# Causal mask of a tile's scores: from a matmul into their bank to VectorE's maximum

## The chip, the core and the metric

One core of a Trainium2 chip runs one layer of a hybrid decoder. The core has five engines, each with its own queue in program order: TensorE (PE; its weight loads are listed as PEld), VectorE (DVE), ScalarE (ACT), GpSimd (POOL) and SyncE (SP, which here issues DMAs alone). TensorE writes only to the eight banks of PSUM (128 partitions by 512 floats each); the others read them out. The metric is device time in microseconds, lower is better.

## What is computed

The layer takes 512 tokens of width 1024. Its first half projects them and runs two groups of heads side by side: a gated recurrence (HGRN2) and a sparse attention (NSA) with a compressed, a selected and a window branch. With 512 tokens both the selected and the window branch come out as plain causal attention, with different keys and values:

```python
m = kpos <= tc[None, None, :, None, None]
sc = jnp.where(m[:, :, None], sc, NEG)
p = jax.nn.softmax(...)
return jnp.einsum('bgrqnl,bgqnld->bgrqd', p.astype(vg.dtype), vg)
```

```python
mw = (kpos <= qpos) & (qpos - kpos < WIN) & (kpos >= 0)
pw = jax.nn.softmax(jnp.where(mw, sw, NEG), axis=-1)
```

There are 8 query heads of 64, in 2 groups with a key head each. The second half of the layer is a gated MLP of width 2816 with a short convolution.

## The kernel before

Tokens are cut into four tiles of 128, i = 0 to 3. Tile i attends to the tiles 0 to i, so a row of its scores has W = (i + 1) * 128 columns. Attention (L1060 and on) is a generator over units. For tiles 0 and 1 a unit is one head with both branches, 2W columns in one bank; for tiles 2 and 3 (the third and fourth) it is one head and one branch, `bs` of length 1, W = 384 or 512 columns. That makes 16 units in each tile of 2 and 3. In between stand a few units of the compressed branch (`h is None`).

Step s of the generator does, in this order: `scores` of unit s; a yield; `flip` of unit s - 4 (LAG = 4); `expo` of unit s; `weigh` of unit s - 1; a yield; and every fourth step `values` of four units.

- `scores` (L969 to L983): two matmuls of float32r inputs, L977 and L978, put the row's scores into a bank S (the keys are kept as a high and a low part). A third, L979, adds the causal mask for the last 128 columns: its weights are an identity, its moving operand `causb`, both bf16, 0 or -1e30 in each element. VectorE's reduction (L981) finds the row's maximum mx, negated.
- `expo` (L985 to L999): ScalarE takes the exponent of S + mx out of the bank, into a tile pt in SBUF, and sums the row (L998).
- `weigh`: at the second of two heads VectorE turns the sums into weights (L1012, L1013) and the rows of both heads are scaled: by VectorE for one branch (L1020), by ScalarE for the other (L1018).
- `flip` (L1029): TensorE transposes pt, 128 columns at a time, into a bank F; ScalarE copies it out to pT (L1036).
- `values` (L1057): products with the values, into a bank oT. `cmp_values` is its counterpart (L1042) in the compressed branch.

`emit` interleaves the generators by hand-set weights. Beside attention run, at 190 to 290 us: projections (`proj_T`, three matmuls a piece through `mm3`, L137 to L139, into a bank pT, with weights that ScalarE and VectorE split into a high part whi, L133, and a low part wlo, L134); the recurrence in levels (`hg_levels`: lev, hgA, hgQ, hgK, hgtot, hgE, L1100 to L1164); and the modulation rows (L1268 to L1287). The order of each engine's queue is the order in which Python emits, so a yield decides what stands beside what.

Banks come from one pool of eight (`PS`); a tile is handed to a later one when its last reader in program order is known. Tiles of more than 256 floats such as pt come from a pool of eight buffers (`TMP`), shared with hgE, hvT and others.

`causb` is made by GpSimd at L1386, ahead of the projections of the keys; GpSimd then computes the roots of the norms (L360).

Of the kernel before, what the change touches and what calls it, by code (L numbers as in the profile page):

```python
# [11 lines left out]
BF16 = mybir.dt.bfloat16  # L12
I32 = mybir.dt.int32
U8 = mybir.dt.uint8
AF = mybir.ActivationFunctionType
ALU = mybir.AluOpType
# [3 lines left out]
P = 128  # L20
# [41 lines left out]
C_CAUS = C_CMASK + NT * 32  # L62
# [30 lines left out]
def hybrid_layer_kernel(ctx: ExitStack, tc: tile.TileContext, d: dict, out: bass.AP, dbg=None):  # L93
    nc = tc.nc
    ve, sc, gp, pe, sp = nc.vector, nc.scalar, nc.gpsimd, nc.tensor, nc.sync

    cst = ctx.enter_context(tc.tile_pool(name="cst", bufs=1))
# [10 lines left out]
    def nm(s):  # L108
        uid[0] += 1
        return f"{s}_{uid[0]}"  # L110
# [4 lines left out]
    def PS(s="ps"):  # L115
        return psum.tile([P, 512], F32, tag="b", name=nm(s))

    def TMP(shape, dt=F32, tag="tmp"):
        n = 1
        for a in shape[1:]:  # L120
            n *= a
        if n > 256:
            return tp.tile(shape, dt, tag="t2", name=nm(tag), bufs=8)
        return tp.tile(shape, dt, tag="t1", name=nm(tag), bufs=4)

    def SM(shape, tag, dt=F32):
        return sm.tile(shape, dt, tag=tag, name=nm(tag))
# [8 lines left out]
    def mm3(o, ah, al, bh, bl, start, stop):  # L136
        pe.matmul(o, ah, bh, start=start, stop=False, skip_group_check=True)  # L137
        pe.matmul(o, ah, bl, start=False, stop=False, skip_group_check=True)  # L138
        pe.matmul(o, al, bh, start=False, stop=stop, skip_group_check=True)  # L139
# [116 lines left out]
    def next_parts(more=True, g=False):  # L256
        if not ahead:
            piece(g)
        w = ahead.pop(0)
        if more:  # L260
            piece()
        return w
# [4 lines left out]
    cb = cst.tile([P, C_COLS], F32, name="cb")  # L267
# [334 lines left out]
    for k in range(KT):  # L602
        h = hT[k]
        n = k + 1
# [28 lines left out]
        for i in range(NT if k else 0):  # L633
            sl = slice(i * P, (i + 1) * P)
# [5 lines left out]
        for j in range(2):  # L640
            sl = slice(j * P, (j + 1) * P)
# [67 lines left out]
    def prep(steps):  # L709

        for step in steps:
            for f, u in [(w[0], w[1:]) for w in step.split()]:
                if f == "s":
                    units[u] = squares(makers[u[0]](int(u[1])))
                elif f == "r":
                    root(units[u])
                elif f == "n":
                    norm(units[u])
                elif f == "f":
                    units[u][0][4](units[u])  # L720
                else:
                    units[u][0][5](units.pop(u))
            yield
# [24 lines left out]
    QS = []  # L748
# [22 lines left out]
    KK = {}  # L771
# [3 lines left out]
    def proj_kv():  # L775
        kva.extend(PS("kva") for _ in range(NT))
        for a in range(0, KT, 2):
            hi, lo = next_parts()
            for b in range(2):
                k = a + b  # L780
                for i in range(NT):
                    sl = slice(i * P, (i + 1) * P)
                    mm3(kva[i], hT[k][:, 0, sl], hT[k][:, 1, sl], hi[:, b], lo[:, b], k == 0, k == KT - 1)
                    if i % 2:
                        yield
# [159 lines left out]
    def cmp_scores(i):  # L945
        ps = PS("S")
        for h in range(8):
            g = h // 4
            pe.matmul(ps[:, h * 64:h * 64 + 64], QS[i][:, h], KC[:, g], start=True, stop=True)
        pv = ps.rearrange("p (h e n) -> p h e n", h=8, e=2)  # L950
        s3 = TMP([P, 8, 32], tag="sc3")
        ve.tensor_tensor(s3, pv[:, :, 0],
                         cb[:, C_CMASK + 32 * i:C_CMASK + 32 * i + 32].unsqueeze(1)
                         .to_broadcast([P, 8, 32]), ALU.add)
        ve.tensor_tensor(s3, pv[:, :, 1], s3, ALU.add)
        mx = SM([P, 8], "cmx")
        ve.tensor_reduce(mx, s3, AX.X, ALU.max)
        ve.tensor_tensor(s3, s3, mx.unsqueeze(2).to_broadcast([P, 8, 32]), ALU.subtract)
        return s3
# [9 lines left out]
    def scores(u):  # L969
        i, h, bs = u  # L970
        if h is None:
            return cmp_scores(i)
        g, W, n = h // 4, (i + 1) * P, len(bs)
        ps = PS("S")
        o = ps[:, 0:n * W].rearrange("p (b j t) -> p j b t", b=n, t=P)
        bsl = slice(bs[0], bs[0] + n)
        pe.matmul(o, QS[i][:, h], KK[g, 0][:, 0:i + 1, bsl], start=True, stop=False)  # L977
        pe.matmul(o, QS[i][:, h], KK[g, 1][:, 0:i + 1, bsl], start=False, stop=False)  # L978
        pe.matmul(o[:, i], identb, causb.unsqueeze(1).to_broadcast([P, n, P]), start=False, stop=True)  # L979
        mx = SM([P, 2], "mx")  # L980
        ve.tensor_reduce(mx[:, 0:n], ps[:, 0:n * W].rearrange("p (b w) -> p b w", b=n), AX.X, ALU.max,  # L981
                         negate=True)
        return ps, mx  # L983

    def expo(u, st):  # L985
        i, h, bs = u
        if h is None:
            sc.activation(st, st, AF.Exp)
            return st
        ps, mx = st  # L990
        W, n = (i + 1) * P, len(bs)
        pt = TMP([P, 512], tag="pt")
        if h % 2 == 0:
            sums[0] = SM([P, 2, 2], "su")
        su = sums[0]
        for e in range(n):
            sl = slice(e * W, (e + 1) * W)
            sc.activation(pt[:, sl], ps[:, sl], AF.Exp, bias=mx[:, e:e + 1], accum_out=su[:, h % 2, e:e + 1])  # L998
        return pt, su  # L999

    def weigh(u, st):
# [58 lines left out]
    def attention(beside):  # L1060
# [5 lines left out]
        for s in range(n + LAG + 1):  # L1066
            if s < n:
                st[s] = scores(us[s])
            yield
            if 0 <= s - LAG < n:  # L1070
                st[s - LAG] = flip(us[s - LAG], st[s - LAG])
            if s < n:
                st[s] = expo(us[s], st[s])
            if 0 <= s - 1 < n:
                st[s - 1] = weigh(us[s - 1], st[s - 1])
            yield
            v = s - LAG - 1
            if v < 0:
                continue
            if us[v][1] is None:  # L1080
                cmp_values(us[v][0], st.pop(v))
                continue
            four.append((us[v], st.pop(v)))
            if len(four) == 4:
                next(beside, None)
                for a in (0, 2):
                    (i, h, bs), even = four[a]
                    values(i, h, bs, even, four[a + 1][1])
                four.clear()
            elif len(four) == 2:  # L1090
                next(beside, None)
# [198 lines left out]
    def ada_cols(s, dst, bias, gain=None):  # L1290
# [3 lines left out]
        for q in range(4):  # L1294
# [5 lines left out]
                late_cols.append((dst, bias, gain))  # L1300
            yield

    adr = hbm.tile([8, D], F32, name="adr")
    late_cols = []

# [78 lines left out]
            yield  # L1384

    gp.tensor_copy(causb, cb[:, C_CAUS:C_CAUS + P])  # L1386
    kv = proj_kv()
    for _ in prep(("sq0 sq1 rq0 rq1",)):
        pass
# [209 lines left out]
    for n, (half, k0, a) in enumerate(steps):  # L1599
# [7 lines left out]
        for i, b in order:  # L1607
            k = k0 + a + b
            sl = slice(i * P, (i + 1) * P)
# [28 lines left out]
```

## Time and profile before

| what | us |
|---|---|
| median of 3 runs (722.7 to 723.0) | 722.96 |
| the profiled execution's own time | 723.01 |
| its span, first to last instruction | 721.2 |
| TensorE busy | 711.8 |
| VectorE busy | 433.6 |
| ScalarE busy | 325.8 |
| attention's scores, starts of the first and the last | 113.5 and 288.0 |

In the profile a line such as L979 is a line of the kernel; `out<-in` names tiles; times are in microseconds, means of one instruction in ns. A timeline row is start, length, engine, line, operation, tiles, shape and count, and in brackets the idle time of the engine before it with what ended it. The chain that ended last is followed from the last instruction back: at each step to what released it, or to the instruction before it on its engine.

### The profile page before, as it was taken

The numbers are of one execution on the slowest core, as the hardware profiler recorded it, in microseconds if no ns is written. First come the engines' busy times: TensorE is split into PE (matmuls) and PEld (weight loads), VectorE is DVE, ScalarE is ACT, GpSimd is POOL, SyncE is SP. The second block draws the span as 40 slices with busy tenths as digits, with TensorE's granted clock in tenths as the row PEclk, the third lists the DMA queues.
The fourth block names the chain that finished last, engine by engine and source line by source line (L and its number), as shares of the span: only waits on it lengthen the run. The fifth ranks groups of instructions, "written<-read, shape, count | busy, mean of one in ns | idle before, by whom it ended". The sixth has DMA issues, their size and how long they took to land.

```text
span 721.2 us, 10429 instructions
## 1 busy us (share of the span) xinstructions
PE 711.8 (99%) x4080; PEld 580.3 (80%) x4080; DVE 433.6 (60%) x828; ACT 325.8 (45%) x626; POOL 107.3 (15%) x99
## 2 busy tenths in 40 slices
PE   8999999999999999999999999999999999999997
PEld 4668898788887777888898888888888888888885
DVE  5688587855767765768845666665555554224223
ACT  5555446655557566424644344444434433211210
POOL 1005020200000000010007627521101101000000
PEclk9999999999999999999999999999999999999999
DMA  9994171465233312724225444543343332225301
GB/s 287 289 269 132 35 231 59 127 206 153 101 119 118 118 59 90 256 68 122 58 60 151 142 116 134 159 116 87 89 118 88 88 117 77 99 88 174 116 31 58
DMA packets 109413, 90.25 MB, mean 125 GB/s; under 512 B 5579, under 2 KB 95275, under 8 KB 109365
## 3 DMA queue, kind: packets, MB, share of 16 engines
q1 hardware_dynamic: 109109, 89.49, 40.8%
q8 instruction: 32, 0.52, 0.3%
q10 hardware_dynamic: 256, 0.11, 0.1%
q14 instruction: 16, 0.13, 0.1%
HBM read 87.46 MB, written 2.13 MB: 124 GB/s over the span
## 4 chain that ended last, share of the span: by engine, by line
PE 88%; DVE 5%; DMA 2%; SPq 2%; ACT 1%; issue 1%; POOL 0%; ACTq 0%; DVEq 0%; POOLq 0%
PE u L138 11%; PE u L139 11%; PE u L137 11%; PE dn L138 6%; PE dn L137 6%; PE dn L139 6%; PE pT L137 3%; PE pT L139 3%; PE pT L138 3%; PE oT L1057 3%; PE F L1029 3%; PE S L977 2%; PE lev L1131 2%; PE oh L137 2%; PE oh L139 2%; PE oh L138 2%
## 5 line engine op out<-in xcount | busy, mean ns | idle before, releaser
L134 DVE TENSOR_TENSOR wlo<-raw,whi 128x1024 fp32r<-128x1024 f32 (+1 forms) x87 | 111.4, 1281 | 145.7 <-ACT whi L133 145.2
L137 PE MATMUL u<-h2h,whi 128*128 128x512 f32 (+1 forms) x360 | 136.7, 380 | 0.0
L138 PE MATMUL u<-h2l,whi 128*128 128x512 f32 (+1 forms) x360 | 136.7, 380 | 0.0
L139 PE MATMUL u<-h2h,wlo 128*128 128x512 f32 (+1 forms) x360 | 136.6, 380 | 0.0
L133 ACT CAST whi<-raw 128x1024 fp32r<-128x1024 f32 (+1 forms) x87 | 89.7, 1031 | 95.0 <-PE dn L139 80.0
L137 PEld LDWEIGHTS u<-h2h,whi 128*128 128x128 f32 x360 | 67.7, 188 | 12.9
L139 PEld LDWEIGHTS u<-h2h,wlo 128*128 128x128 f32 x360 | 67.7, 188 | 12.7
L138 PEld LDWEIGHTS u<-h2l,whi 128*128 128x128 f32 x360 | 67.7, 188 | 12.7
L138 PE MATMUL dn<-wlo,gT 128*128 128x512 f32 x160 | 62.3, 390 | 0.0
L139 PE MATMUL dn<-whi,gT 128*128 128x512 f32 x160 | 62.3, 389 | 0.0
L137 PE MATMUL dn<-whi,gT 128*128 128x512 f32 x160 | 62.2, 389 | 0.0
L1544 POOL TENSOR_TENSOR y<-y,y 128x512 f32<-128x512 f32 x22 | 28.3, 1288 | 165.0 <-DVE y L1539 165.0
L360 POOL TENSOR_TENSOR hrs<-hrs,mhalf 128x4 f32<-128x4 f32 (+2 forms) x16 | 17.7, 1124 | 223.5 <-DVE hrs L359 223.5
L133 ACT CAST gT<-y 128x512 fp32r<-128x512 f32 x20 | 12.4, 621 | 71.6 <-POOL y L1544 71.6
L998 ACT ACTIVATE pt<-S,mx 128x128 f32<-128x128 f32 (+3 forms) x64 | 33.8, 534 | 17.6 <-DVE mx L981 15.1
L137 PE MATMUL pT<-hT,whi 128*128 128x512 f32 x96 | 41.3, 430 | 0.0
L134 DVE TENSOR_TENSOR gT<-y,gT 128x512 fp32r<-128x512 f32 x20 | 14.9, 743 | 43.3 <-ACT gT L133 43.3
L139 PE MATMUL pT<-hT,wlo 128*128 128x512 f32 x96 | 37.8, 394 | 0.0
L138 PE MATMUL pT<-hT,whi 128*128 128x512 f32 x96 | 37.5, 391 | 0.0
L981 DVE TENSOR_REDUCE mx<-S 128x1 f32<-128x384 f32 (+3 forms) x48 | 28.4, 596 | 14.6 <-PE S L979 14.6
L1542 ACT ACTIVATE y<-y 128x512 f32<-128x512 f32 x22 | 13.9, 632 | 49.6 <-DVE y L1539 49.6
L138 PEld LDWEIGHTS dn<-wlo,gT 128*128 128x128 f32 x160 | 30.0, 188 | 6.4 <-DVE wlo L134 0.2
(346 smaller groups left out, 1437.9 us busy)
## 6 DMA issues: line engine op xcount, KB each, us to landing
raw<-in_w_up SPq DMA_DIRECT2D x44, 512.0 KB, 4.1
aw<-in_w_ada SPq DMA_DIRECT2D x12, 1024.0 KB
raw<-in_w_down SPq DMA_DIRECT2D x10, 1024.0 KB, 4.9
ada<-in_w_ada SPq DMA_DIRECT2D x32, 256.0 KB, 5.6
raw<-in_w_in SPq DMA_DIRECT2D x7, 1024.0 KB, 5.2
x<-in_x SPq DMA_DIRECT2D x8, 512.0 KB, 5.2
raw<-in_w_cmp SPq DMA_DIRECT2D x8, 512.0 KB
raw<-in_w_out SPq DMA_DIRECT2D x4, 1024.0 KB, 8.6
```

Of the source, the lines that this page charges most:

```text
L133: sc.copy(hi, src)
L134: (eng or ve).tensor_tensor(lo, src, f32(hi), ALU.subtract)
L137: pe.matmul(o, ah, bh, start=start, stop=False, skip_group_check=True)
L138: pe.matmul(o, ah, bl, start=False, stop=False, skip_group_check=True)
L139: pe.matmul(o, al, bh, start=False, stop=stop, skip_group_check=True)
L360: gp.tensor_tensor(o, o, mhalf[:, 0:n], ALU.pow)
L977: pe.matmul(o, QS[i][:, h], KK[g, 0][:, 0:i + 1, bsl], start=True, stop=False)
L981: ve.tensor_reduce(mx[:, 0:n], ps[:, 0:n * W].rearrange("p (b w) -> p b w", b=n), AX.X, ALU.max, negate=True)
L998: sc.activation(pt[:, sl], ps[:, sl], AF.Exp, bias=mx[:, e:e + 1], accum_out=su[:, h % 2, e:e + 1])
L1029: pe.transpose(ps[:, j * P:(j + 1) * P], src[:, j * P:(j + 1) * P], ident)
L1057: pe.matmul(oTs[i][r:r + 64, h // 2], VV[:, j, b, g], src[:, q * P:(q + 1) * P], start=(h == 0 and b == 0 and j == 0), stop=False, skip_gr ...
L1544: gp.tensor_tensor(ys[0], ys[0], y, ALU.mult)
```

## The change

Units of tiles 2 and 3 get their mask from VectorE. The matmul L979 and its weight load go for them. The maximum and the mask become one instruction, `tensor_tensor_reduce`: it reads the bank and a mask of 384 zeros and 128 columns of 0 or -1e30 (the last W columns of `cmask`), writes -(S + mask) to pt in SBUF, and gives the minimum of what it wrote, which is the negated maximum. ScalarE then takes the exponent in place, pt to pt, with a scale of -1. So the bank S has VectorE as its last reader, and pt is taken in `scores` instead of `expo`. Tiles 0 and 1 keep the matmul. The mask is set up by GpSimd with a fill and a copy behind `causb`.

```diff
         pe.matmul(o, QS[i][:, h], KK[g, 0][:, 0:i + 1, bsl], start=True, stop=False)
-        pe.matmul(o, QS[i][:, h], KK[g, 1][:, 0:i + 1, bsl], start=False, stop=False)
+        pe.matmul(o, QS[i][:, h], KK[g, 1][:, 0:i + 1, bsl], start=False, stop=(n == 1))
+        mx = SM([P, 2], "mx")
+        if n == 1:
+            pt = TMP([P, 512], tag="pt")
+            ve.tensor_tensor_reduce(pt[:, 0:W], ps[:, 0:W], cmask[:, 512 - W:512], -1.0, 1e30, ALU.add, ALU.min,
+                                    mx[:, 0:1])
+            return pt, mx
         pe.matmul(o[:, i], identb, causb.unsqueeze(1).to_broadcast([P, n, P]), start=False, stop=True)
-        mx = SM([P, 2], "mx")
         ve.tensor_reduce(mx[:, 0:n], ps[:, 0:n * W].rearrange("p (b w) -> p b w", b=n), AX.X, ALU.max,
                          negate=True)
         return ps, mx
...
-        pt = TMP([P, 512], tag="pt")
+        pt = ps if n == 1 else TMP([P, 512], tag="pt")
...
-            sc.activation(pt[:, sl], ps[:, sl], AF.Exp, bias=mx[:, e:e + 1], accum_out=su[:, h % 2, e:e + 1])
+            sc.activation(pt[:, sl], ps[:, sl], AF.Exp, bias=mx[:, e:e + 1], scale=(-1.0 if n == 1 else 1.0),
+                          accum_out=su[:, h % 2, e:e + 1])
...
+    cmask = cst.tile([P, 512], BF16, name="cmask")
...
     gp.tensor_copy(causb, cb[:, C_CAUS:C_CAUS + P])
+    gp.memset(cmask[:, 0:384], 0.0)
+    gp.tensor_copy(cmask[:, 384:512], cb[:, C_CAUS:C_CAUS + P])
```

## The prediction

> **What bounds the kernel now.** I read the page first, then the busy time in stretches, then the groups and the timelines of the stretch in which the changed instructions run.
>
> ```profile
> span 721.2 us, 10429 instructions
> ...
> PE 711.8 (99%) x4080; PEld 580.3 (80%) x4080; DVE 433.6 (60%) x828; ACT 325.8 (45%) x626; POOL 107.3 (15%) x99
> ...
> PE 88%; DVE 5%; DMA 2%; SPq 2%; ACT 1%; issue 1%; POOL 0%; ACTq 0%; DVEq 0%; POOLq 0%
> ```
>
> TensorE is busy for 99% of the span, and it holds 88% of the chain that ended last. The changed instructions lie between 189 and 288 us, so that stretch decides. The columns of the next view are stretch, length, and busy time with count of PE, PEld, DVE, ACT and POOL, then the granted clock and the DMA.
>
> ```profile
> 188.00:288.00 100.00, 99.83 (x817) 77.37 (x815) 69.78 (x165) 63.17 (x148) 0.00 (x0) 1.00 0.31 100
> 320.00:721.00 401.00, 396.51 (x1835) 330.88 (x1833) 211.12 (x271) 147.71 (x213) 78.25 (x61) 1.00 0.35 105
> ```
>
> There TensorE is busy for 99.83 of 100 us at the full granted clock, VectorE for 69.78, ScalarE for 63.17, GpSimd not at all. Ends of matmuls are modelled, so I price TensorE by the distance from one start to the next, never by a duration. The second row says that what TensorE gains in attention has no reason to be lost later: 396.51 of 401 us are busy behind it, and the transfers' share is 0.35.
>
> **What is removed.** 32 mask matmuls with their weight loads: the program's order of the changed kernel has the 16 units of tile 2 and the 16 of tile 3 without them, and TensorE's order is otherwise the same. What follows a removed one is a projection matmul pT (8 times), the recurrence's lev of L1131 (6 times), or a transpose-like group: F, two of lev L1156, one of ps (18 times).
>
> ```profile
> L979 PE MATMUL S<-causb,identb 128*128 128x128 bf16 x32 | 7.4, 230 | 0.0
> ```
>
> The 230 ns are a latency; the starts tell the price. Timeline of TensorE: start, length, line.
>
> ```profile
> 188.44 0.40 PE L137 MATMUL pT<-hT,whi 128*128 128x512 f32 x1
> 188.68 0.39 PE L138 MATMUL pT<-hT,whi 128*128 128x512 f32 x1
> ...
> 205.71 0.34 PE L978 MATMUL S<-KK,qs 128*128 128x384 f32 x1
> 205.88 0.23 PE L979 MATMUL S<-causb,identb 128*128 128x128 bf16 x1
> 205.92 0.48 PE L137 MATMUL pT<-hT,whi 128*128 128x512 f32 x1
> 206.24 0.40 PE L138 MATMUL pT<-hT,whi 128*128 128x512 f32 x1
> ...
> 219.63 0.39 PE L139 MATMUL pT<-hT,wlo 128*128 128x512 f32 x1
> 219.87 0.49 PE L1029 MATMUL F<-cb,pt 128*128 128x128 f32 x3
> 220.11 0.42 PE L977 MATMUL S<-KK,qs 128*128 128x384 f32 x1
> ...
> 231.23 0.34 PE L977 MATMUL S<-KK,qs 128*128 128x384 f32 x1
> 231.41 0.34 PE L978 MATMUL S<-KK,qs 128*128 128x384 f32 x1
> 231.59 0.23 PE L979 MATMUL S<-causb,identb 128*128 128x128 bf16 x1
> 231.65 0.50 PE L1029 MATMUL F<-cb,pt 128*128 128x128 f32 x3
> 231.91 0.47 PE L137 MATMUL pT<-hT,whi 128*128 128x512 f32 x1
> ```
>
> Before a pT: from the start of L978 at 205.71 to that of the second pT matmul at 206.24 are 0.53 us. The mask's own step is only 0.04 (205.88 to 205.92); the pT behind it takes 0.32 to the next start, where one inside its stream takes 0.24 (188.44 to 188.68). Without the mask L978 takes 0.18, as L977 does ahead of another matmul of its kind (231.23 to 231.41), and the pT 0.24: 0.42 together, 0.11 saved. Before an F: 231.41 to 231.91 are 0.50; without it 0.18, then the three transposes in 0.24, as behind L139 (219.87 to 220.11): 0.08 saved.
>
> For lev the chain of waits gives the whole group of eight, in the order start, length:
>
> ```profile
> 215.23 0.89 PE lev L1131 x8
> ...
> 224.13 0.95 PE lev L1131 x8
> ```
>
> Behind a mask (the second row) it takes 0.06 more, and the mask's own step another 0.06 (231.59 to 231.65): 0.12. The 512-wide tiles of tile 3 are taken at the same prices. Sum: 8 x 0.11 + 6 x 0.12 + 18 x 0.08 = 3.0 us of TensorE.
>
> By the Trainium skill, TensorE: Matmul & The Clock Gate, section Back-to-back issue gap, a matmul of 128 columns costs 134 cycles of 2.4 GHz, 0.056 us, when its weight load is hidden; 32 of them would be 1.8 us. The rows agree for the mask's own step (0.04 to 0.06), and differ on the matmul behind it, which no sentence of that section prices; I go by the rows.
>
> **What is added on VectorE.** The reduction becomes an addition with a running minimum that writes all its elements, and a second short instruction that writes the minimum out: the program's order has 32 more rows there. Groups of VectorE and of ScalarE in 185 to 290 us, with count, busy us and mean ns of one, then the idle time before:
>
> ```profile
> L981 DVE TENSOR_REDUCE mx<-S 128x1 f32<-128x512 f32 x16 | 10.9, 685 | 6.2 <-PE S L979 6.2
> L981 DVE TENSOR_REDUCE mx<-S 128x1 f32<-128x384 f32 x16 | 8.8, 552 | 3.6 <-PE S L979 3.6
> ...
> L1013 DVE TENSOR_TENSOR su<-su,gates 128x2 f32<-128x2 f32 x15 | 2.4, 162 | 0.5
> ...
> L1113 DVE TENSOR_TENSOR hgA<-lev,cb 128x512 f32<-128x512 f32 x2 | 1.4, 684 | 0.0
> ```
>
> The trace has no such instruction. Nearest is L1113, a two-operand instruction that also reads a bank and writes 512 floats: 684 ns, against 685 for the reduction. So from below the long one costs nothing more (it streams the same elements and more operands, so a gain is excluded), and the short one at most what L1013 takes, 162 ns, and less where it follows at once. From above it runs over its elements twice: 0.55 or 0.68 more, and the 0.16. I take 0.1 each, since L1113 is the nearest in every respect: 3.2 us in all, against 100 - 69.8 = 30.2 us of idle VectorE, which is the cover; without it the 3.2 us would come on the path.
>
> **ScalarE** reads the exponent's argument from SBUF instead of a bank.
>
> ```profile
> L998 ACT ACTIVATE pt<-S,mx 128x512 f32<-128x512 f32 x16 | 11.1, 694 | 5.8 <-DVE mx L981 3.3 <-DVE su L1012 2.4
> ...
> L1018 ACT ACTIVATE pt<-pt,su 128x512 f32<-128x512 f32 x6 | 4.0, 713 | 0.0
> ```
>
> L1018 does that already: 713 against 694 ns, 0.02 more each, 0.6 in all, under ScalarE's 36.8 us of idle time.
>
> **Waits that move.** The scores' bank is now free after VectorE's instruction, not after the exponent. The tile pt is taken a step earlier; in VectorE's order two of the 32 new instructions get a wait for the transposes that read the buffer last. Those transposes stand directly behind the scores in TensorE's order, so each waits for one such group (0.24 us above). Behind them in VectorE's queue stand the recurrence's L1140 and L1147, for which a later lev waits; VectorE's idle time lets them catch up.
>
> **Where TensorE meets a chain.** Two places in the stretch have nothing to spare. PE, ACT and DVE timelines:
>
> ```profile
> 194.72 0.66 PE L1029 MATMUL F<-cb,pt 128*128 128x128 f32 x4 [0.17 <-ACT pT L1036]
> 195.29 0.45 PE L977 MATMUL S<-KK,qs 128*128 128x384 f32 x1
> ...
> 209.61 0.55 PE L1029 MATMUL F<-cb,pt 128*128 128x128 f32 x3
> ```
> ```profile
> 194.09 0.58 ACT L1036 COPY pT<-F 128x512 f32<-128x512 f32 x1
> 194.57 0.58 ACT L998 ACTIVATE pt<-S,mx 128x384 f32<-128x384 f32 x1
> ...
> 208.94 1.12 ACT L1018 ACTIVATE pt<-pt,su 128x384 f32<-128x384 f32 x2 [1.43 <-DVE su L1013]
> ```
> ```profile
> 200.19 0.56 DVE L981 TENSOR_REDUCE mx<-S 128x1 f32<-128x384 f32 x1 [1.35 <-PE S L979]
> ...
> 204.45 1.22 DVE L134 TENSOR_TENSOR wlo<-raw,whi 128x1024 fp32r<-128x1024 f32 x1 [3.03 <-ACT whi L133]
> ...
> 206.19 0.55 DVE L981 TENSOR_REDUCE mx<-S 128x1 f32<-128x384 f32 x1
> ```
>
> At 194.72 F waits for the copy pT, and the scores at 195.29 for the exponent that ends at 195.15, whose bank they take. In the changed order F needs nothing so late, and those scores wait for that same copy, which ends at 194.67: they can start 0.48 earlier. At 209.61 F starts just behind the first of the two weighings of L1018 (two in 1.12 us from 208.94), and this goes back through the queues of ScalarE and VectorE to the scores of 200.19; VectorE's two new instructions there add 0.2, the one ahead of that copy another 0.1, and the pT behind 195.29 gives 0.11. So F comes 0.48 + 0.11 - 0.3 = 0.3 us earlier, whatever TensorE saves ahead of it. Seven of the removed ones stand before that point (2 lev, 3 pT, 2 F: 0.73), and they are lost in waiting; 25 behind it count, 3.0 - 0.7 = 2.3. Between 0 (the short instruction costs its full 162 ns and the bank brings less) and 0.6 for this place, I take 0.3.
>
> **Setting up the mask** adds a fill of 128x384 and a copy on GpSimd, behind L1386.
>
> ```profile
> 59.17 0.29 POOL L1386 CAST causb<-cb 128x128 bf16<-128x128 f32 x1
> ...
> 64.61 3.23 POOL L360 TENSOR_TENSOR hrs<-hrs,mhalf 128x8 f32<-128x8 f32 x2 [1.88 <-DVE hrs L359]
> ```
>
> The copy is another L1386, 0.29; the fill, three times its elements, at most 0.9. GpSimd next idles 1.88 us ahead of 64.61, which covers 1.2; without that cover the same 1.2 us would reach the rotary work of the queries. Cost 0. No DMA is added, removed or moved: SP's order is the same.
>
> **Sum.** 2.3 + 0.3 = 2.6 us. Against the profiled execution's own 723.01 us (span 721.2 and 1.8 around it; the median of the runs is 722.96): **720.4 us**.
>
> **The rivals.**
> First, only the mask's own step goes, and the weight load behind it stays as exposed as it is: 0.04 for the five pT of the 25, 0.06 for the 20 others, 1.4 us, and 0.3: 721.3 us. For it: the exposed 0.08 on the pT could belong to the scores' switch of kind, not to the mask's. Against it: behind L139, which is a matmul of the same kind as L978, F and pT follow without it. The skill's figure of 0.056 us gives the same 1.4 for 25.
>
> Second, the chain from scores to F binds all through tile 2, as at 209.61: only tile 3's 16 count (1 lev, 4 pT, 11 F: 1.44), and the short instruction's 0.16, twice in each of the four lags of tile 2, costs 1.3: 722.9 us. For it: two tight places within 20 us. Against it: the row of 188 to 288 us leaves 0.17 us of idle TensorE, so there are not many.
>
> Third, slower: VectorE becomes the bound because the new instruction takes twice the time of L1113, 0.55 + 0.16 or 0.68 + 0.16 more, 16 x 0.71 + 16 x 0.84 = 25 us. Of the 30.2 idle, 6.2 + 3.6 stand directly ahead of the reductions, waiting for TensorE, and can't take it up: 20.4 remain, 4.6 us come on the path, and 3.0 are saved: 724.6 us. It decides from about (20.4 + 3.0) / 32 = 0.73 us more each. Vector Engine (DVE) Microarchitecture Reference of the Trainium skill, Points that are easy to get wrong, says that an instruction of this family with two sources in SBUF that aren't bf16 runs at half rate, for want of a port for the accumulator; here one source is a bank and the mask is bf16, so by its own condition it does not hold, and no run here shows it.
>
> Last, that the change doesn't do what it says: the program's order shows the 32 pairs gone, so all that is left of it is that the work behind 288 us takes nothing over; 723.0 us.
>
> **How the numbers follow.** Forecast 720.4, chance 0.58; first rival 721.3 with 0.14; second 722.9 with 0.13; third 724.6 with 0.13; last 0.02. The forecast's own range is 719.3 (the place gives 0.6, all 3.0 count) to 721.2. The range, 719.3 to 723.0, leaves out the third. A measurement here tells 0.2%, 1.45 us, from no change: faster is below 721.5, slower above 724.4. Faster: 0.58 and two thirds of the first, 0.67; same: the rest of the first, the second, the last and a tail of the third, 0.22; slower 0.11.
>
> **What would show it.** Right: L978 to the second pT start 0.42, to the end of a three-fold F 0.42; the new instruction within 0.05 us of the reduction and the short one at or under 0.16; the scores at 195.29 earlier by about half a microsecond; a new wait of TensorE near 209 us and none of that size behind it. Wrong: a new instruction over 1 us, TensorE's idle time from 210 to 288 us above 1 us, or starts that stay 0.5 apart.

## The result, and the profile after

The changed kernel takes 720.27 us (median of 6 runs, 719.99 to 721.07) against 722.83 us before (6 runs, 722.66 to 723.5): a ratio of 0.9965 with a 95% interval of 0.9952 to 0.9978. It is faster by 2.56 us.

The page of the changed kernel, its first lines and its chain:

```profile
span 718.3 us, 10396 instructions
...
PE 708.9 (99%) x4048; PEld 582.4 (81%) x4048; DVE 434.0 (60%) x860; ACT 326.4 (45%) x626; POOL 108.2 (15%) x101
...
PE 86%; DVE 6%; ACT 2%; DMA 2%; SPq 2%; issue 1%; POOL 0%; ACTq 0%; POOLq 0%; DVEq 0%
```

The 32 matmuls are gone (4080 to 4048) and TensorE is busy for 2.9 us less. VectorE has 32 instructions more and only 0.4 us more to do. The groups of VectorE in 185 to 290 us, then those of ScalarE:

```profile
L982 DVE CUSTOM_DVE_ANT_0 pt<-S,cmask 128x512 f32<-128x512 f32 x16 | 10.9, 686 | 5.2 <-PE S L978 5.2
L982 DVE CUSTOM_DVE_ANT_0 pt<-S,cmask 128x384 f32<-128x384 f32 x16 | 8.9, 554 | 2.2 <-PE S L978 1.9 <-PE ps L1202 0.2
L982 DVE DVE_READ_ACCUMULATOR2_ANT mx<- 128x1 f32 x32 | 2.7, 84 | 0.0
```
```profile
L1003 ACT ACTIVATE pt<-pt,mx 128x512 f32<-128x512 f32 x16 | 11.6, 726 | 6.1 <-DVE mx L982 3.7 <-DVE su L1018 2.4
```

The instruction that adds the mask takes 686 and 554 ns, the reduction took 685 and 552. The read-out of the minimum (84 ns) is not even queued: VectorE's timeline shows the instruction behind it starting at the same time.

```profile
190.24 0.55 DVE L982 CUSTOM_DVE_ANT_0 pt<-S,cmask 128x384 f32<-128x384 f32 x1
190.71 0.08 DVE L982 DVE_READ_ACCUMULATOR2_ANT mx<- 128x1 f32 x1
190.71 0.69 DVE L1119 TENSOR_TENSOR hgA<-lev,cb 128x512 f32<-128x512 f32 x1
```

TensorE's timeline has the step as forecast: from L978 to the second matmul of pT 0.46 us for 512 columns (254.81 to 255.27), where the kernel before takes 0.59 (254.95 to 255.54). For 384 columns it is 0.42 (206.53 to 206.95), the forecast's own figure.

```profile
254.14 0.60 PE L1035 MATMUL F<-cb,pt 128*128 128x128 f32 x4
254.50 0.48 PE L977 MATMUL S<-KK,qs 128*128 128x512 f32 x1
254.81 0.39 PE L978 MATMUL S<-KK,qs 128*128 128x512 f32 x1
255.04 0.39 PE L137 MATMUL pT<-hT,whi 128*128 128x512 f32 x1
255.27 0.40 PE L138 MATMUL pT<-hT,whi 128*128 128x512 f32 x1
```
```profile
254.95 0.40 PE L978 MATMUL S<-KK,qs 128*128 128x512 f32 x1
255.18 0.23 PE L979 MATMUL S<-causb,identb 128*128 128x128 bf16 x1
255.22 0.48 PE L137 MATMUL pT<-hT,whi 128*128 128x512 f32 x1
255.54 0.39 PE L138 MATMUL pT<-hT,whi 128*128 128x512 f32 x1
```

**Where the time came from, place by place.** TensorE's order is the same in both but for the masks, so the start of each scores' first matmul (L977 in PE's timeline) can be compared one by one. The table gives how much earlier (minus) it starts than in the kernel before, at six places named by their start before, less the same figure at 189.49, the first of tile 2: the profiled runs come to that point up to 0.6 us apart from the kernel before, which has nothing to do with tiles 2 and 3. The other rows are the experiments below.

| kernel | 195.29 | 207.63 | 211.09 | 264.01 | 267.22 | 285.26 |
|---|---|---|---|---|---|---|
| changed | -0.56 | -1.01 | -0.71 | -2.42 | -1.98 | -2.47 |
| before, no mask at all | -0.01 | -0.46 | -0.20 | -1.91 | -1.63 | -2.09 |
| changed, mask matmul kept | -0.54 | -0.57 | -0.50 | -0.50 | -0.50 | -0.50 |
| changed, masked scores back in the bank | 0.01 | -0.44 | -0.15 | -1.88 | -1.38 | -1.85 |
| changed, hgE a step later | -0.74 | -1.21 | -1.44 | -3.04 | -3.12 | -3.59 |
| before, hgE a step later | -0.54 | -0.57 | -0.66 | -0.67 | -0.67 | -0.67 |
| changed, one more element copied | -0.50 | -0.94 | -0.51 | -2.08 | -1.64 | -2.13 |
| changed, addition and reduction apart | 0.01 | -0.45 | 1.01 | 3.72 | 5.54 | 5.98 |
| changed, unread maximum behind | -0.10 | -0.55 | 0.67 | 1.09 | 2.50 | 2.00 |

In the changed kernel the figure falls by 0.11 to 0.14 at a mask ahead of a pT or lev and by 0.06 to 0.10 ahead of an F or its like, 3.1 for all 32, and rises at two places. The first is the one near 209 us, foreseen; PE's row names ScalarE's weighing:

```profile
208.57 0.55 PE L1035 MATMUL F<-cb,pt 128*128 128x128 f32 x3 [0.30 <-ACT pt L1024]
```

The second, at 262 us, was not foreseen. PE, DVE and ACT timelines of the changed kernel:

```profile
261.71 0.60 PE L1035 MATMUL F<-cb,pt 128*128 128x128 f32 x4
262.23 0.39 PE L1291 MATMUL ps<-rhl,onesr 128*128 128x256 f32 x1
262.69 0.38 PE L1292 MATMUL ps<-rhl,onesr 128*128 128x256 f32 x1
```
```profile
260.82 0.42 DVE L1141 TENSOR_TENSOR hgK<-hgK,hgtot 128x256 f32<-128x256 f32 x1
262.21 0.42 DVE L1288 SCALAR_TENSOR_TENSOR rhl<-rows,rhl 128x256 fp32r<-128x256 f32 x1 [0.97 <-ACT rhl L1287]
```
```profile
261.28 0.62 ACT L1106 COPY hgE<-hgK 128x512 f32<-128x512 f32 x1 [0.83 <-DVE hgK L1141]
261.80 0.38 ACT L1287 ACTIVATE rhl<-rows 128x256 fp32r<-128x256 f32 x1
```

The products of the modulation rows need rhl: its high part from ScalarE, its low part from VectorE. ScalarE's L1287 stands behind the copy hgE, which waits for VectorE's L1141; VectorE's L1288 waits for ScalarE in turn, and L1292 starts after 262.63. Before, the same chain ended at 264.31 + 0.42 = 264.73, and the product that reads the low part started at 265.11: 0.38 us to spare, which TensorE's gain has used up. From F to the products and on to L1063 the steps are now 0.52, 0.46 and 0.31 us, where they were 0.36, 0.20 and 0.21: 0.52 us are lost (0.44 in the table, where a mask's step is gained in the same stretch). The view of idle time shows no wait here, since the ends of matmuls are modelled; only the starts do.

```profile
264.31 0.42 DVE L1282 SCALAR_TENSOR_TENSOR rhl<-rows,rhl 128x256 fp32r<-128x256 f32 x1 [0.97 <-ACT rhl L1281]
```
```profile
265.11 0.28 PE L1286 MATMUL ps<-rhl,onesr 128*128 128x256 f32 x1
```

### The profile page after: what moved, and what is told of

Its sections match the earlier page's. It is cut to its first block, busy times and chain, and to the rows that moved or that the text cites. A ratio compares the mean times of both kernels' runs of the same rounds, so it can differ in the third digit from the quotient of the medians.

```text
span 718.3 us, 10396 instructions
## 1 busy us (share of the span) xinstructions
PE 708.9 (99%) x4048; PEld 582.4 (81%) x4048; DVE 434.0 (60%) x860; ACT 326.4 (45%) x626; POOL 108.2 (15%) x101
## 3 DMA queue, kind: packets, MB, share of 16 engines
HBM read 87.46 MB, written 2.13 MB: 125 GB/s over the span
## 4 chain that ended last, share of the span: by engine, by line
PE 86%; DVE 6%; ACT 2%; DMA 2%; SPq 2%; issue 1%; POOL 0%; ACTq 0%; POOLq 0%; DVEq 0%
PE u L139 11%; PE u L137 11%; PE u L138 11%; PE dn L138 6%; PE dn L137 6%; PE dn L139 6%; PE pT L137 3%; PE pT L139 3%; PE pT L138 3%; PE oT L1063 2%; PE F L1035 2%; PE oh L137 2%; PE oh L139 2%; PE oh L138 2%; PE S L977 2%; PE rows L1274 2%
## 5 line engine op out<-in xcount | busy, mean ns | idle before, releaser
L138 PE MATMUL u<-h2l,whi 128*128 128x512 f32 (+1 forms) x360 | 136.8, 380 | 0.0
L139 PE MATMUL u<-h2h,wlo 128*128 128x512 f32 (+1 forms) x360 | 136.8, 380 | 0.0
L139 PEld LDWEIGHTS u<-h2h,wlo 128*128 128x128 f32 x360 | 67.7, 188 | 12.8
L138 PEld LDWEIGHTS u<-h2l,whi 128*128 128x128 f32 x360 | 67.7, 188 | 12.8
L138 PE MATMUL dn<-wlo,gT 128*128 128x512 f32 x160 | 62.3, 390 | 0.0
L139 PE MATMUL dn<-whi,gT 128*128 128x512 f32 x160 | 62.3, 389 | 0.0
L139 PE MATMUL pT<-hT,wlo 128*128 128x512 f32 x96 | 37.9, 394 | 0.0
L138 PE MATMUL pT<-hT,whi 128*128 128x512 f32 x96 | 37.6, 392 | 0.0
L138 PEld LDWEIGHTS dn<-wlo,gT 128*128 128x128 f32 x160 | 30.0, 188 | 6.3 <-DVE wlo L134 0.2
L137 PEld LDWEIGHTS dn<-whi,gT 128*128 128x128 f32 x160 | 30.1, 188 | 6.3
L139 PEld LDWEIGHTS dn<-whi,gT 128*128 128x128 f32 x160 | 30.0, 188 | 6.2
```

## The experiments

Each kernel ran on the same chip as a set of runs of the kernel before, whose median there was 723.03 or 723.09 us.

**The masks' steps alone.** The kernel before, with L979 left out for tiles 2 and 3.

```diff
-        pe.matmul(o[:, i], identb, causb..., start=False, stop=True)
+        if n > 1:
+            pe.matmul(o[:, i], identb, causb..., start=False, stop=True)
```

> The kernel before with the mask matmul of tiles 2 and 3 left out (the output lacks the causal mask there); reduction, exponent and the bank of the scores as before. It tells how much of the gain is TensorE's 32 steps alone. Theory (steps of 0.08 to 0.12 us go, those ahead of 209 us are lost in a wait, half a microsecond is lost at the products of the adaptive rows at 262 us, and the scores at 195 us still wait for the exponent): 25 steps of 2.3 us, less 0.5, plus about 0.1 = 1.9 us under before, 720.9 us, 0.6 slower than the changed kernel. Rival one (only the mask's own 0.04 to 0.06 us goes): 1.4 less 0.2 = 1.2 us under before, 721.6 us. Rival two (all 32 steps come through, no wait takes any): 3.0 us under before, 719.8 us, faster than the changed kernel.

Measured: 720.79 us, ratio 0.9969 (0.9957 to 0.998), 2.2 under before. In the table nothing is gained at 195.29, then the steps come, and 2.09 us stand at the end. So TensorE's steps carry most of the gain, and they are worth more than the mask's own 0.04 to 0.06 us: the theory holds, the first rival (721.6) and the second (719.8) fall.

**The bank alone.** The changed kernel with the mask matmul kept.

```diff
-        pe.matmul(o, ..., start=False, stop=(n == 1))
+        pe.matmul(o, ..., start=False, stop=False)
+        pe.matmul(o[:, i], identb, causb..., start=False, stop=True)
```

> The changed kernel with the mask matmul kept as well (the mask is added twice). TensorE's steps are those of before; what is left of the change is the bank that comes free after VectorE's instruction, and VectorE's new instruction. Theory: only the 0.5 us at 195 us is gained, 722.3 us (0.3 to 0.7 under before). Rival (the gain came from the bank and the order of waits, the mask's steps were hidden): 720.3 us as the changed kernel. Second rival (VectorE's new work costs time by itself): not under before, 722.8 to 723.3 us.

Measured: 722.71 us, ratio 0.9996 (0.9988 to 1.0005). By the times alone this is no change, and the second rival can't be told from the theory. The starts can tell: 0.54 us are gained in one step at 195.29, and 0.50 are kept to the end. That is the bank. The time under before (0.32) is at the lower end of what the theory gave. The rival that the masks' steps were hidden is out by 2.4 us.

**The bank held again.** The new instruction writes its sums back into the bank, and the exponent reads them there.

```diff
-            ve.tensor_tensor_reduce(pt[:, 0:W], ps[:, 0:W], cmask..., mx[:, 0:1])
-            return pt, mx
+            ve.tensor_tensor_reduce(ps[:, 0:W], ps[:, 0:W], cmask..., mx[:, 0:1])
+            return ps, mx
...
```

> The changed kernel, with VectorE's instruction writing the masked scores back into the bank and the exponent reading them there: the bank is held until the exponent ends, as before, and the exponent reads what it read before. Theory: the scores near 195 us wait for the exponent again, 0.5 us later than in the changed kernel, and nothing behind gives it back: 720.8 us. Rival (the early release of the bank is worth nothing, since the wait near 209 us takes it anyway): 720.3 us. Second rival (writing into the bank makes VectorE's instruction longer than 0.69 us): over 721 us, and the row of the instruction shows it.

Measured: 721.33 us, ratio 0.9976 (0.9965 to 0.9987), 1.1 over the changed kernel. The table has 0.01 instead of -0.56 at 195.29 and 0.62 less at the end, which is the theory's half microsecond. The other 0.4 is not explained by it: the kernel before was itself 0.2 slower beside this run (723.03 for 722.83), and the profiled run was already 0.56 us later than the changed kernel's at 189.49, ahead of the first edited instruction. By their ratios the two kernels' intervals overlap, so it is the starts that tell them apart. VectorE's groups:

```profile
L981 DVE CUSTOM_DVE_ANT_0 S<-S,cmask 128x512 f32<-128x512 f32 x16 | 11.1, 696 | 5.2 <-PE S L978 5.2
...
L981 DVE DVE_READ_ACCUMULATOR2_ANT mx<- 128x1 f32 x32 | 4.5, 141 | 0.0
```

Into the bank the instruction takes 10 ns more and the read-out 141 instead of 84, too little for the second rival.

**VectorE at twice the price.** Addition and reduction as two instructions.

```diff
-            ve.tensor_tensor_reduce(pt..., ps..., cmask..., -1.0, 1e30, ALU.add, ALU.min, mx[:, 0:1])
+            ve.tensor_tensor(pt[:, 0:W], ps[:, 0:W], cmask[:, 512 - W:512], ALU.add)
+            ve.tensor_reduce(mx[:, 0:1], pt[:, 0:W], AX.X, ALU.max, negate=True)
...
```

> The changed kernel with the one VectorE instruction replaced by two, an addition of the mask into the tile and a reduction of the tile; all else as changed. It doubles VectorE's cost for the mask: about 0.5 to 0.6 us more in each of 32, some 17 us in all. Theory (VectorE stays under the 0.73 us each from which it would bound; only the tight places at 195, 209 and 262 us lose, about 0.5 each as one more instruction stands in each chain): 721.3 to 722 us. Rival one (VectorE's idle time takes it all): 720.3 us. Rival two (VectorE becomes the bound already): 724 us or more, with TensorE's idle time between 188 and 288 us above 3 us.

Measured: 729.17 us, ratio 1.0085 (1.0072 to 1.0099): slower than before, and 8.9 over the changed kernel. The theory falls. Busy time in 188 to 290 us (PE, PEld, DVE, ACT, POOL), and PE's waits:

```profile
188.00:290.00 102.00, 95.20 (x746) 76.18 (x745) 83.95 (x187) 60.94 (x141) 0.00 (x0) 1.00 0.28 94
```
```profile
PE F L1034 <- ACT pt L1023: 3.1, 3, 1.5
PE oT L1062 <- ACT pT L1041: 1.6, 2, 1.0
PE ps L1290 <- ACT rhl L1286: 1.3, 1, 1.3
```

TensorE idles 6.8 of 102 us, 6.0 of them in these six waits for ScalarE. Two of the six are the places near 209 and 262 us (1.45 and 1.28 us); the other four, 0.6 to 1.0 us each, are places where the changed kernel doesn't wait. The theory had counted on the tight places alone. Time and idle time are those of rival two, but VectorE is not full: 18 us of it are idle. It does not bind by its busy time; its idle time lies where it waits for others and can't take the work up.

**The same work, outside the row's chain.** A maximum over constants, of the same width, behind each new instruction.

```diff
             ve.tensor_tensor_reduce(pt..., ps..., cmask..., mx[:, 0:1])
+            ve.tensor_reduce(causb[:, 0:1], cb[:, 0:W], AX.X, ALU.max)
```

> The changed kernel with a second VectorE instruction behind each of the 32 new ones: a maximum over a constant row of the same width, whose result nobody reads. It is as much VectorE work as in the run with addition and reduction apart (0.55 to 0.69 us each, 19.7 us), but the row's own maximum doesn't wait for it. It tells why that run lost 8.9 us although VectorE had 18 us of idle time left between 188 and 290 us. Theory one (the queue: everything behind on VectorE, rotations of the recurrence, weights of the rows, comes late, whoever the work belongs to): 727 to 730 us. Theory two (the row's own chain from scores to transposes got longer by the second instruction): 720.3 to 722 us.

Measured: 724.95 us, ratio 1.0027 (1.0016 to 1.0038). The 19.7 us of work cost 4.7 us; neither theory has it alone. So about half of the 8.9 us is the queue, whoever the work belongs to. The two runs differ in little but the row's own maximum standing one instruction further back; that the rest goes with it is argued, not shown. The place near 209 us shows the queue. VectorE's timeline, then ScalarE's and PE's row:

```profile
206.52 0.55 DVE L982 CUSTOM_DVE_ANT_0 pt<-S,cmask 128x384 f32<-128x384 f32 x1
...
206.99 0.55 DVE L984 TENSOR_REDUCE causb<-cb 128x1 bf16<-128x384 f32 x1
207.45 1.31 DVE L1147 COPY_PREDICATED hgA<-cb,lev 128x512 f32<-128x512 uint8 x1
...
209.49 0.16 DVE L1020 TENSOR_TENSOR su<-su,gates 128x2 f32<-128x2 f32 x1
211.44 0.69 DVE L134 TENSOR_TENSOR mixN<-oT,mixN 128x512 fp32r<-128x512 f32 x1 [1.79 <-ACT mixN L133]
```
```profile
209.75 1.12 ACT L1025 ACTIVATE pt<-pt,su 128x384 f32<-128x384 f32 x2 [1.87 <-DVE su L1020]
```
```profile
210.41 0.55 PE L1036 MATMUL F<-cb,pt 128*128 128x128 f32 x3 [1.23 <-ACT pt L1025]
```

VectorE runs without a gap up to the weights su, ScalarE's weighings wait for them, and F for the weighings; right behind su VectorE idles 1.79 us. That idle time is in the sum of idle time and of no use to F.

**A short instruction behind each.** A copy of one element a row in its place.

```diff
+            ve.tensor_copy(causb[:, 0:1], cb[:, 0:1])
```

> The changed kernel with a copy of one element a row behind each of the 32 new VectorE instructions, result unread: the short extra instruction of some 0.1 to 0.16 us that the prediction had charged to VectorE and that the read-out of the maximum did not cost. Theory (only the tight places lose, twice the copy near 209 us and once or twice near 262 us): 0.3 to 0.6 over the changed kernel, 720.7 us. Rival (hidden wholly in VectorE's idle time): 720.3 us.

Measured: 720.42 us, ratio 0.9964 (0.9952 to 0.9977), 0.15 over the changed kernel, no difference that the times can show. The copy lasts 152 ns and moves what follows by 0.07:

```profile
222.15 0.15 DVE L984 CAST causb<-cb 128x1 bf16<-128x1 f32 x1
222.22 0.16 DVE L1019 RECIPROCAL su<-su 128x2 f32<-128x2 f32 x1
```

The table shows 0.2 less behind the place near 209 us (-0.51 for -0.71) and another 0.14 by 264 us. The 0.34 at the end lies in the theory's range (0.3 to 0.6), but only the starts tell theory and rival apart.

**What makes the matmul behind the mask late.** The kernel before, the mask once as a float32r matmul of 128 columns, once as a bf16 matmul over all columns of the row (`cmask`, zeros but for the last 128).

```diff
-        pe.matmul(o[:, i], identb, causb..., start=False, stop=True)
+        if n == 1:
+            pe.matmul(o[:, i, 0], identr, causr, start=False, stop=True)
...
```
```diff
-        pe.matmul(o[:, i], identb, causb..., start=False, stop=True)
+        if n == 1:
+            pe.matmul(ps[:, 0:W], identb, cmask[:, 512 - W:512], start=False, stop=True)
...
```

> The kernel before with the mask of tiles 2 and 3 as a float32r matmul of the same 128 columns, the kind of the scores' own matmuls. It tells what makes the matmul behind the mask start 0.08 us late. If it is the switch of kind (bf16 to float32r): from the mask's start to the second matmul behind it 0.24 + its own step, the late 0.08 gone. If it is the short matmul that doesn't cover the next weight load: the matmul behind stays 0.08 late, about 0.31 us from its start to the next start.

> The kernel before with the mask of tiles 2 and 3 as a bf16 matmul over all columns of the row (384 or 512, zeros but for the last 128), so that the kind still switches but the matmul is long. If the late 0.08 us comes from the short matmul: the matmul behind takes 0.23 from its start to the next start, and the mask's own step grows to 0.16 to 0.23. If it comes from the switch of kind: it keeps 0.31. The time grows by 32 times 0.05 to 0.15 over before, 724 to 727 us.

Measured (one run each): 722.95 and 726.34 us. PE's timeline of the first:

```profile
255.28 0.22 PE L981 MATMUL S<-causr,identr 128*128 128x128 f32 x1
255.34 0.44 PE L137 MATMUL pT<-hT,whi 128*128 128x512 f32 x1
255.62 0.39 PE L138 MATMUL pT<-hT,whi 128*128 128x512 f32 x1
```

Then the weight loads (PEld) behind the mask, in the kernel before and in the wide form:

```profile
255.19 0.20 PEld L137 LDWEIGHTS pT<-hT,whi 128*128 128x128 f32 x1
255.31 0.19 PEld L138 LDWEIGHTS pT<-hT,whi 128*128 128x128 f32 x1
255.54 0.19 PEld L139 LDWEIGHTS pT<-hT,wlo 128*128 128x128 f32 x1
```
```profile
256.92 0.20 PEld L137 LDWEIGHTS pT<-hT,whi 128*128 128x128 f32 x1
257.15 0.19 PEld L138 LDWEIGHTS pT<-hT,whi 128*128 128x128 f32 x1
257.38 0.19 PEld L139 LDWEIGHTS pT<-hT,wlo 128*128 128x128 f32 x1
```

Mask and first pT together take 0.36 before (255.18 to 255.54), 0.34 in the same kind, and 0.46 in the wide form (256.92 to 257.38), which is twice the 0.23 of any 512-column matmul here: nothing is late behind it, although the kind switches. The start of a matmul behind a bf16 one is recorded early (255.22 before, 256.96 in the wide form), so the mask's step can't be read from the matmuls. The loads show it: the load of a matmul's weights starts with the matmul ahead of it (in the kernel before, L139's load and L138 itself both at 255.54); the bf16 mask's own load is the exception and starts with the mask, at 255.18. So the mask takes 0.12 (255.19 to 255.31) and the pT behind it 0.23, and in the wide form both take 0.23, as the second expectation has it. The lateness comes with the short matmul, not with the switch of kind, which is worth 0.02 at most.

What the short matmul fails to cover is not shown by a run of its own. The record speaks for the next weight load: ahead of a pT or lev, where a mask costs 0.11 to 0.14, that load is recorded as 0.19 to 0.20 us long; ahead of an F, where it costs 0.06 to 0.10, it is 0.14 (L1029's loads, 141 ns in the mean).

**The wait at 262 us taken away.** In the recurrence hgE is issued behind the yield instead of ahead of it.

```diff
-            if 2 * L < P:
-                E = early_keys(KS, 2 * L)
             yield
+            if 2 * L < P:
+                E = early_keys(KS, 2 * L)
```

> The changed kernel with the recurrence's copy hgE issued one step later, so that the copy rhl of the modulation rows, at 261 us, no longer stands behind it in ScalarE's queue. Theory (the half microsecond lost at 262 us comes from that order): the two products there start without a wait, 0.3 to 0.5 us under the changed kernel, 719.9 us. Rival (the level's next product then waits for hgE, or the wait turns up a few microseconds later): 720.3 us or more.

Measured: 719.54 us, ratio 0.9949 (0.9935 to 0.9962), 0.7 under the changed kernel. ScalarE's timeline now has the copy rhl ahead of hgE:

```profile
260.63 0.37 ACT L1287 ACTIVATE rhl<-rows 128x256 fp32r<-128x256 f32 x1
...
263.22 0.60 ACT L1106 COPY hgE<-hgK 128x512 f32<-128x512 f32 x1
```

The place at 262 us loses nothing (-3.04 to -3.12), and neither does the one near 209, which the theory had not claimed. The last start is 1.1 us earlier than in the changed kernel: 0.2 of it come at 195.29, 0.5 near 209 and 0.5 at 262, and 0.13 are lost again between 257 and 261 us, where F (256.33 in this run's own time) now starts just behind the first of ScalarE's two weighings. So part of what the rival said is there too, a wait that turns up elsewhere.

**The same move without the change.** The kernel before, hgE a step later.

> The kernel before, mask by matmul, with the recurrence's copy hgE issued one step later, as in the run that took 0.7 us off the changed kernel. Theory (the waits near 209 and 262 us show only because TensorE has become faster; before, the products at 262 us started with 0.4 us to spare): 722.9 us, within 0.3 of before. Rival (the later copy is a gain of its own): 0.5 to 1 us under before, 722.2 us.

Measured: 722.56 us, ratio 0.9992 (0.9983 to 1.0001), 0.5 under before at an interval that just reaches 1. The theory is right that nothing is won at 262 us (-0.67 on both sides of it) and next to nothing near 209 (0.09). But 0.54 are won at 195.29. ScalarE's copy and exponent, for which F and those scores wait, stood behind hgE there too (timeline of the kernel before):

```profile
193.56 0.62 ACT L1100 COPY hgE<-hgK 128x512 f32<-128x512 f32 x1 [2.34 <-DVE hgK L1135]
```

So most of this is a gain of its own, as the rival has it, and it is the same wait that the bank's release removes: the two gains of 0.54 don't add up. The 3.59 us of the run before this one are the masks' steps up to that start, 3.05, and the 0.67 here, less the 0.13 lost again.

**The first two tiles as well.** All masks on VectorE, two instructions for a unit with both branches.

```diff
-        if n == 1:
...
-        pe.matmul(o[:, i], identb, causb..., start=False, stop=True)
-        ve.tensor_reduce(mx[:, 0:n], ps..., AX.X, ALU.max, negate=True)
-        return ps, mx
+        pt = TMP([P, 512], tag="pt")
+        for e in range(n):
+            sl = slice(e * W, (e + 1) * W)
+            ve.tensor_tensor_reduce(pt[:, sl], ps[:, sl], cmask..., mx[:, e:e + 1])
+        return pt, mx
...
```

> The changed kernel, with the mask of the first and second tile moved to VectorE as well (two instructions per unit, one for each branch; 16 more mask matmuls are gone). Theory (each mask's step is 0.08 to 0.12 us of TensorE, and TensorE has little idle time from 113 to 188 us, where VectorE has over 40 us): 16 times 0.1 = 1.6 us, of which a wait may take a part: 0.5 to 1.6 under the changed kernel, 719.2 us. Rival (that stretch waits for other chains, and the two shorter instructions of VectorE stand in them): 720.3 us as the changed kernel, or more.

Measured: 720.45 us, ratio 0.9965 (0.9952 to 0.9977): as the changed kernel. PE's waits up to 160 us:

```profile
PE cps L892 <- DMA raw<-in_w_cmp: 1.1, 1, 1.1
PE F L1032 <- DVE pt L1023: 0.5, 1, 0.5
```

Neither is in the changed kernel. Each mask gives its 0.1 (against the changed kernel the scores gain 0.5 from 113 to 124 us and 0.9 from 146 to 189 us), but what is saved ahead of 141 us, and about 0.8 more, goes in these two waits, most of it in that for the weights of the compression: their load was issued at 137.0 us in this run, 1.1 later than in the changed kernel. So the rival's first half holds, waits for other chains. This profiled run was also 1 us late at 113 us, by a wait for a load at 29 us, which the edit does not touch; how much of the late issue comes from that is open.

**The second tile, with hgE later.** Seven of the eight masks that go more stand behind that load (the first is at 139 us). The loop over the branches is that of the run before.

```diff
-        if n == 1:
+        if i > 0:
...
```

> The changed kernel with hgE one step later and the mask of the second token tile on VectorE as well; the first tile keeps its matmul. Eight more mask matmuls are gone, all from 146 us on, behind the load of the compression's weights that took the gain of the first tile's in the run with all tiles. Theory (0.11 us each come through): 0.5 to 0.9 under the kernel with hgE alone moved, 718.8 us. Rival (the two VectorE instructions per unit or the next load take it): 719.5 us.

Measured: 718.59 us, ratio 0.9937 (0.9925 to 0.995), 0.95 under the kernel with hgE moved and 4.4 under before: the fastest of all. The seven masks give 0.09 to 0.14 us each from 146 to 189 us, and in 188 to 290 us the view counts no idle time of TensorE:

```profile
188.00:290.00 102.00, 102.00 (x856) 84.16 (x858) 74.57 (x213) 68.75 (x156) 0.00 (x0) 1.00 0.35 115
```

## Why the prediction was right

The forecast was 2.6 us, measured are 2.56 by the medians and 2.47 by the starts from 189 us to 285.26 (about 2.54 with the step of the last mask, which stands behind). As forecast, nothing of it is lost later: the profiled runs are 2.89 us apart at 290 us and 2.95 at the end. The mechanism was right in its main terms, but two terms were off by about 0.4 and 0.5, and it is luck that they cancel.

- **TensorE's steps, 3.0 us: right.** The starts give 0.11 to 0.14 ahead of a pT or lev and 0.06 to 0.10 ahead of an F or its like, for 0.11, 0.12 and 0.08; together 3.1. The run with hgE later lets all but 0.13 of the sum come through. The first rival (the exposed part stays) falls with the run without masks. The mask with its lateness costs 0.11 to 0.14 ahead of a pT, and that is what other short matmuls cost: four of F and the late L977 behind them take 0.67 (254.14 to 254.81), less 0.23 for a matmul of 512 columns 0.44, 0.11 each. By the Trainium skill, TensorE: Matmul & The Clock Gate, LDWEIGHTS (loading the stationary operand), a weight load takes P / 1.2 ns for P columns, an estimate of 0.107 us for 128; the trace agrees with a step of that size, though it records each load as 0.19 or 0.14 long. The prediction had looked at the 0.056 us of the section Back-to-back issue gap, which the page gives without a weight load, and was wrong that the section prices no more: for pairs of load and matmul it gives 0.081 us at 128 columns, an estimate of 2.6 us for 32, under the 3.1 measured. No run shows why it is only 0.06 to 0.10 ahead of an F; the shorter weight load there is the candidate.
- **VectorE, 0.1 us each: the size was off, it is about 0.** The long instruction came within 2 ns of the reduction, as taken, and the read-out was below the bound of 0.16, but it overlaps its neighbours completely. The run with the copied element shows what a short instruction costs when it is queued: 0.07 each. The forecast had put this work under 30.2 us of idle VectorE; with next to nothing to hide, that cover was hardly tried. It is worth less than it looked: the copied element, 0.07 each, already costs 0.34 by the last start, and the run with two instructions loses 8.9 us.
- **The place near 209 us, 0.3 us: the size was off, it gave 0.71.** It had been charged with three short instructions of 0.1 that were not there; without them its own terms give 0.59. With real ones of 0.07 it is 0.51. The other 0.1 is a little of the steps ahead of the place, which the forecast had called lost: in the run without masks the place gives 0.20, where the forecast's terms leave the pT's 0.11. The mechanism is as forecast: weighing after weights, F after weighing.
- **The bank at 195 us, 0.48: right.** 0.54 when alone, 0.56 in the changed kernel with the mask's step of 0.13 ahead of it, and its wait is now for the copy pT. With the bank held again it goes.
- **The steps behind 209 us, 2.3 us with no further wait: the term that was missed.** The steps came (0.71 to 2.42, and 1.98 to 2.47), and 0.52 was lost at 262 us. "None of that size behind it" was wrong, and the trace of before could have warned: a chain with 0.38 us to spare is at risk from a gain of 2.4.
- **ScalarE and GpSimd: hidden, as said.** The exponent takes 0.03 more (726 for 694 ns); GpSimd's idle time behind the mask's setup shrank from 1.88 to 0.96 us.
- **The third rival's deciding point, 0.73 us each, was too high.** The instruction didn't double. But at 0.55 to 0.69 more, the run with two instructions lost 8.9 us where that sum leaves nothing to lose. What failed there is counting 20.4 us of VectorE's idle time as cover: 18 us were idle in that run while TensorE stood still for 6.8.
- **The range.** Its lower end is 0.1 too low by its own terms: 723.0 less 3.6 is 719.4.

## What to carry to other kernels

Where one engine is full, list ahead of time the chains that reach it with less to spare than the gain you expect: they take their part, and one of them here took half a microsecond that a one-line move of another copy gave back. An engine's idle time is cover only if it lies between the added work and the one who waits for its result; two instructions for one cost 8.9 us with 18 us idle. Work on a full TensorE is best priced by the distance of starts with and without it, the matmul behind it included.

## What the runs showed of the hardware

- A matmul of 128 columns ahead of one of 512 costs 0.11 to 0.14 us, about half of a 512-column one (0.23), whether bf16 or float32r, and 0.06 to 0.10 ahead of a group of 128-column transposes; a switch of kind alone showed no more than 0.02. The weight load of a float32r matmul is recorded as starting with the matmul ahead of it (255.54 us for both), which gives the step where a matmul's start is recorded early.
- VectorE's addition with a running minimum over a bank and a bf16 row, writing 512 floats, takes 686 ns, as long as the plain reduction (685). Its read-out (84 ns) overlaps the instruction behind it; after the same instruction writing into a bank it is 141 ns.
- ScalarE's exponent of 512 floats takes 726 ns out of SBUF in place and 694 out of a bank.
